# Layer 1's third adaLN projection on VectorE, and its merge with tokens on the partitions

## The chip, the cores and the metric

The kernel runs on one core of a Trainium2 chip. The core has TensorE (PE; its weight loads are shown apart, as PEld), VectorE (DVE), ScalarE (ACT) and GpSimd (POOL). SyncE (SP) issues the DMAs, in order. The metric is the device time of one execution, in microseconds (us). The kernel before takes 1507.12 us, the median of 3 runs (1506.59 to 1509.21).

## The reference

Two layers of a transformer block act on 256 latent tokens and 256 context tokens of width 1024. Each layer is

```
sh1, sc1, g1, sh2, sc2, g2 = split(silu(c) @ w_ada + b_ada, 6)      # adaLN, one row per stream
h = x * (1 + sc1) + sh1
qA, kA, vA, qB, kB, vB, xr, yr, g = split(h @ w_in)
ya = windowed attention(qA, kA, vA);  yb = global attention(qB, kB, vB)
yc = (forward scan + backward scan of a gated recurrence over conv(xr)) * gelu(yr)
ga, gb, gc = split(sigmoid(g), 3)
o = (ga * (ya @ w_br_a) + gb * (yb @ w_br_b) + gc * (yc @ w_br_c)) @ w_out
x = layernorm(ALPHA * x + g1 * o)
x = layernorm(ALPHA * x + g2 * (relu((x * (1 + sc2) + sh2) @ w_ff1) ** 2 @ w_ff2))
```

Layer 1 returns the latent stream alone, so its queries, gates, merge and MLP run on 256 tokens, while layer 0 runs them on 512. All data is fp32.

## The kernel before, in words

**Units.** Each weight is cut into units of up to 1 MB, listed once in `plan_units` in the order of use. A unit is loaded into one of three raw buffers (`emit_dma`), split into a high and a low fp32r part in four pieces (`queue_split`: ScalarE, in the recurrence also VectorE, writes `whi`; VectorE writes `wlo = raw - whi`), and multiplied in three matmuls per 128 rows (high by high, high by low, low by high). `take` hands out a unit; `prefetch` then loads two or three units ahead and queues the split of the next. `tick`, called after every three matmuls, issues one piece at every third call. TensorE waits when a piece that it needs is late.

**Two forms of product.** `cm` keeps a 128x128 block of the weight in TensorE and streams the tokens past it: the result has channels on the partitions, and for layer 1 each matmul streams 256 columns (`LAT`). `unit`, used for `w_out` and `w_ff2`, keeps 128 tokens of the activation in TensorE and streams 512 weight columns: the result has tokens on the partitions. Weights for it are "wide" units of 512 rows by 512 columns.

**adaLN in the background.** A projection of 2048 columns (`ada_queue`) is eight loads of 1 MB into the same three raw buffers. With `dve` set, each load is followed by eight VectorE instructions (the first load by multiplications, line 291, the others by multiply-adds into eight accumulators, line 293), and at the end 16 short matmuls sum over the partitions (`sums`). Without it, TensorE multiplies each load itself in a step of eight recorded matmuls (`mms`). `ada_step`, called at each prefetch, issues the next load once `self.pe`, the kernel's own running estimate of TensorE time at build, has passed `ada_at`, and sets that to `self.pe` plus `ADA_PACE` of the projection's layer (line 326). The adds are issued by `tick` from 3000 ns of that estimate after the load, spread over the rest of the pace; those left over are issued ahead of the next load. `mm` adds 0.42 ns per column to the estimate, so a unit of layer 0's MLP, 48 matmuls of 512 columns, counts 10.3 us. The table `ADA` (line 328) says where a projection is queued: two for layer 1 at the start of layer 0's MLP, and a third (`ga1`, blocks 8 to 11, which give the MLP's scale and gate) on TensorE at layer 1's first gate.

**Layer 1's merge.** While `attention` runs, `pair` fills TensorE's gaps with `filler`: the queries of branch B, then `merge_gates` and `merge_branch` per branch, in the order of `MERGE[1]`. Both use `cm`: 12 gate units of 48 matmuls, four units of 48 for branch c, and eight of 24 for branches a and b, 960 matmuls of 256 columns in all. The gate product goes through a tanh on ScalarE; the branch product is multiplied by it and summed on VectorE, and the sum `m` is split for `wout`. `tail_units` runs the last two `w_out` units and the LayerNorm (`ln_z`), transposes the result (`ln_t`) and makes the MLP's input (`ln_h`).

**Order.** The instructions of an engine stand in one queue, which a scheduler fills at build time; at run time each queue is strictly in order.

Of the kernel before, what the change touches and what calls it, by code (L numbers as in the profile page):

```python
# [9 lines left out]
F32R = mybir.dt.float32r  # L10
AF = mybir.ActivationFunctionType
ALU = mybir.AluOpType
# [3 lines left out]
KD = D // 128  # L16
SEQ = 256
# [9 lines left out]
COL = dict(qA=0, kvA=512, qB=768, kvB=1280, xr=1536, yr=2560, g=3584)  # L27
# [20 lines left out]
class Kern:  # L48
# [95 lines left out]
    def plan_units(self):  # L144
        a, U = self.a, []

        def cols(w, c0, r0=0, k=KD):
            return w[r0:r0 + 128 * k, c0:c0 + 256].rearrange("(k p) c -> p k c", p=128)

        def wide(w, c0, r0):  # L150

            return w[r0:r0 + 512, c0:c0 + 512].rearrange("(k p) c -> p k c", p=128)

        for l in range(DEPTH):
            win = a["w_in"][l]
            order = ("xr0 yr0 xr1 yr1 xr2 yr2 xr3 yr3 kvA qA0 kvB qA1 qB0 qB1",
                     "xr0 xr1 yr0 yr1 kvA xr2 yr2 kvB xr3 yr3 qA0 qA1 qB0 qB1")[l]
            for n in order.split():
                key = (n,) if n[:2] == "kv" else (n[:2], int(n[2]))
                U.append(((l,) + key, cols(win, COL[key[0]] + 256 * sum(key[1:])), KD))  # L160
            for what, br in self.MERGE[l]:
                for n in range(4):
# [12 lines left out]
        self.units = U  # L175
        self.u_dma = self.u_split = 0
        self.u_cur = -1
        self.raw, self.wt = {}, {}
        self.pieces = deque()
# [8 lines left out]
            self.u_dma += 1  # L188

    def is_wide(self, i):  # L190
        return self.units[i][0][1] in ("wo", "f2")

    def shaped(self, t, i):

# [74 lines left out]
    def ada_queue(self, l, blocks, dve):  # L269
# [48 lines left out]
        for k in range(KD):  # L318
            if dve:
                self.ada_q.append((lambda k=k: dma(k),  # L320
                                   [lambda k=k, j=j, s=s: add(k, j, s) for j in range(4) for s in range(2)],
                                   sums if k == KD - 1 else None, self.ADA_PACE[l]))
            else:
                self.ada_q.append((lambda k=k: dma(k), [], lambda k=k: mms(k), 0.0))

    ADA_PACE = (9500, 18000)

    ADA = (('bra0',0,4,1),('bra0',0,8,1),('mlp0',1,0,1),('mlp0',1,4,1),('ga1',1,8,0))

    def ada_start(self, at):  # L330
        for a, l, b, dve in self.ADA:
# [792 lines left out]
    def merge_gates(self, l, br):  # L1124

        cols = BOTH if l == 0 else LAT
        self.tg[br] = []
        for n in range(4):
            w = self.take((l, "g", br, n))
            if br == "c":  # L1130
                if n == 1:
                    while any(step[2] for step in self.bg):
                        self.bg_step()
                    self.y["C"] = []
                    yc = [t for _ in range(KD // 2) for t in self.g2(l, "yc")]
                    for c in range(KD):
                        self.nc.sync.dma_start(out=yc[c][:, cols], in_=self.ycd[c][:, cols])
                elif n > 1:
                    for c in range(4 * n - 8, 4 * n - 4):
                        hi, lo = self.g2(l, "yc_hl", F32R)  # L1140
                        self.split(hi[:, cols], lo[:, cols], yc[c][:, cols], "a")
                        self.y["C"].append((hi, lo))
                    if n == 3:
                        self.flags.add((l, "y", "C"))
            for b, t in enumerate(self.g2(l, "tg")):
                yield from self.cm(w, self.h, cols, b)
                self.act(t[:, cols], self.out, AF.Tanh, scale=0.5)
                self.tg[br].append(t)

    def merge_branch(self, l, br, first, last):  # L1150
        nc = self.nc
        cols = BOTH if l == 0 else LAT
        k = KD if br == "c" else KD // 2
        while (l, "y", br.upper()) not in self.flags:
            yield "need"
        ys = self.y.pop(br.upper())
# [133 lines left out]
    def tail_units(self, l, which, keys, xs):  # L1290


        final = l and which == 2
# [3 lines left out]
            self.hn = [(self.g("h_hi", F32R), self.g("h_lo", F32R)) for _ in range(KD)]  # L1297
        if l:
            ws = []
            for tb, j in ((2, 0), (2, 1), (3, 0), (3, 1)):  # L1300
                if tb == 2:
                    ws.append(self.take(keys[j]))
                self.unit(keys[j], ws[j], xs, (tb,), True)
                if j and not final:
                    self.ln_z(tb)
                elif j:
                    self.output(tb)
# [42 lines left out]
    def wout(self, l):  # L1350
        self.start_residual(l, 1)
        if l == 0:
            self.load_x(l)
        for h in range(2):
            self.unit((l, "wo", 0, h), self.take((l, "wo", 0, h)), self.m_hl(), self.tbs, True)
        self.tail_units(l, 1, [(l, "wo", 1, 0), (l, "wo", 1, 1)], self.m_hl())
        self.m = {}

# [112 lines left out]
    def layer(self, l):  # L1471
        a = self.a
        self.ada_start("layer%d" % l)
        self.layer_consts(l)
        self.ks, self.qs, self.qt, self.vv, self.y, self.m, self.tg, self.qs_at = {}, {}, {}, {}, {}, {}, {}, {}
        self.lru(l)
        if l == 0:
# [122 lines left out]
```

## Time and profile before

| | us |
|---|---|
| median of 3 runs | 1507.12 |
| the profiled execution | 1507.38 |
| its span in the trace | 1505.6 |
| PE busy | 1455.2 |
| DVE busy | 1154.4 |
| ACT busy | 772.2 |
| POOL busy | 292.7 |

The trace covers the span; 1.8 us of the profiled execution's time lie around it. Layer 0's MLP runs from about 575 to 940 us, layer 1's recurrence with its projections from there to about 1109, attention and merge to 1285, `w_out` to 1306, and layer 1's MLP to the end. A busy share counts the time in which an engine had an instruction in work, also where that instruction ran slower than elsewhere.

### The profile page before, as it was taken

Reading aid. Unit: us, or ns where it says so; the run is one execution under the profiler, and the core shown is the slowest. Engines: PE = TensorE matmul, PEld = TensorE weight load, DVE = VectorE, ACT = ScalarE, POOL = GpSimd, SP = SyncE. Lnnn points to the kernel's source line nnn. Section 1 sums busy time; section 2 is a strip of 40 time slices with the busy share of each in tenths; the row PEclk is TensorE's granted clock in tenths of the full one; section 3 lists DMA queues with packets and bytes.
Section 4 is the critical chain, followed back from the end, with each engine's and each line's share of the span. In section 5 each row is a group of like instructions: output and inputs, shape, how many; then the busy total and the mean of one; then the engine's idle time right before and its main releaser. Section 6 shows DMA issues by size and latency. Waiting matters only on the chain.

```text
span 1505.6 us, 22308 instructions
## 1 busy us (share of the span) xinstructions
PE 1455.2 (97%) x8364; PEld 1226.5 (81%) x8364; DVE 1154.4 (77%) x2179; ACT 772.2 (51%) x1594; POOL 292.7 (19%) x298
## 2 busy tenths in 40 slices
PE   7899999999999999899999999999899999899997
PEld 4688988777878879678878887897787899799986
DVE  4699987758688966977657768888989577886666
ACT  2698667565223327313323234587777655655452
POOL 0533422100000002711110301264411003031110
PEclk9999999999999999999999999999999999999999
DMA  9523310105557552444435343342345735755563
GB/s 325 194 85 111 113 57 29 43 29 172 169 190 247 198 198 95 159 160 159 162 112 192 116 168 110 107 143 74 123 144 178 243 109 185 251 169 186 181 193 112
DMA packets 156748, 225.69 MB, mean 150 GB/s; under 512 B 5840, under 2 KB 118992, under 8 KB 151520
## 3 DMA queue, kind: packets, MB, share of 16 engines
q1 hardware_dynamic: 156640, 224.27, 45.2%
q8 instruction: 65, 1.06, 0.3%
q14 instruction: 43, 0.35, 0.1%
HBM read 218.97 MB, written 5.28 MB: 149 GB/s over the span
## 4 chain that ended last, share of the span: by engine, by line
PE 80%; DVE 12%; ACT 4%; issue 2%; DMA 1%; POOL 0%; SPq 0%; DVEq 0%; ACTq 0%
PE ps_cm L92 42%; PE ps_tm L92 26%; DVE wlo L128 3%; PE ps_s L92 2%; PE ps_pv L92 2%; PE ps_pT L99 2%; PE ps_ada L92 2%; PE ps_gate L92 2%; DVE ada_acc L293 1%; DVE xc L647 1%; DMA raw_ada<-in_w_ada_dram 1%; PE ps_qT L99 1%; ACT L103 1%; DVE lru_q L718 1%; DVE lru_i L708 0%
## 5 line engine op out<-in xcount | busy, mean ns | idle before, releaser
L120 ACT CAST whi<-raw 128x512 fp32r<-128x512 f32 x521 | 300.1, 622 | 374.0 <-PE ps_tm L92 195.3
L128 DVE TENSOR_TENSOR wlo<-raw,whi 128x512 fp32r<-128x512 f32 x560 | 407.0, 753 | 103.2 <-ACT whi L120 98.0
L92 PE MATMUL ps_cm<-h_hi,wlo 128*128 128x256 f32 (+1 forms) x1216 | 406.9, 337 | 7.0 <-DVE wlo L128 6.9
L92 PE MATMUL ps_cm<-h_hi,whi 128*128 128x256 f32 (+1 forms) x1216 | 408.5, 340 | 3.0 <-ACT whi L120 2.0
L92 PE MATMUL ps_cm<-h_lo,whi 128*128 128x256 f32 (+1 forms) x1216 | 406.1, 336 | 0.2 <-POOL h_lo L1249 0.2
L92 PEld LDWEIGHTS ps_cm<-h_hi,whi 128*128 128x128 f32 x1216 | 230.4, 191 | 39.9 <-ACT whi L120 7.1
L92 PEld LDWEIGHTS ps_cm<-h_hi,wlo 128*128 128x128 f32 x1216 | 231.9, 191 | 34.3 <-DVE wlo L128 9.2
L92 PEld LDWEIGHTS ps_cm<-h_lo,whi 128*128 128x128 f32 x1216 | 232.0, 191 | 24.1 <-POOL h_lo L1249 0.7
L293 DVE SCALAR_TENSOR_TENSOR ada_acc<-raw_ada,silu,ada_acc 128x512 f32<-128x512 f32 x224 | 168.7, 799 | 49.6 <-DMA raw_ada<-in_w_ada_dram 49.4
L92 PE MATMUL ps_tm<-wlo,f_hi 128*128 128x512 f32 x384 | 150.2, 392 | 2.1 <-DVE wlo L128 2.1
L92 PE MATMUL ps_tm<-whi,f_hi 128*128 128x512 f32 x384 | 149.7, 390 | 0.0
L92 PE MATMUL ps_tm<-whi,f_lo 128*128 128x512 f32 x384 | 149.3, 389 | 0.0
L1188 POOL TENSOR_TENSOR x<-x,res 128x512 f32<-128x512 f32 x36 | 51.9, 1445 | 306.8 <-DVE res L1187 306.8
L92 PE MATMUL ps_tm<-wlo,h_hi 128*128 128x256 f32 x320 | 92.0, 287 | 6.1 <-DVE wlo L128 6.0
L92 PE MATMUL ps_tm<-whi,h_hi 128*128 128x256 f32 x320 | 92.9, 290 | 1.2 <-ACT lru_r L103 0.6
L92 PE MATMUL ps_tm<-whi,h_lo 128*128 128x256 f32 x320 | 91.4, 286 | 0.0
L92 PEld LDWEIGHTS ps_tm<-wlo,f_hi 128*128 128x128 f32 x384 | 72.1, 188 | 19.6 <-DVE wlo L128 5.2
L92 PEld LDWEIGHTS ps_tm<-whi,f_hi 128*128 128x128 f32 x384 | 72.1, 188 | 15.7 <-ACT whi L120 0.8
L103 ACT ACTIVATE p<-ps_s,mx 128x512 f32<-128x512 f32 (+1 forms) x96 | 58.5, 618 | 51.2 <-DVE mx L1001 29.9
L92 PEld LDWEIGHTS ps_tm<-whi,f_lo 128*128 128x128 f32 x384 | 72.1, 188 | 14.8
L685 POOL TENSOR_TENSOR lru_i<-lru_i,xc 128x512 f32<-128x512 f32 x32 | 52.8, 1680 | 89.3 <-ACT lru_i L103 89.3
L92 PEld LDWEIGHTS ps_tm<-wlo,h_hi 128*128 128x128 f32 x320 | 62.0, 194 | 7.7 <-DVE wlo L128 7.3
(173 smaller groups left out, 2449.5 us busy)
## 6 DMA issues: line engine op xcount, KB each, us to landing
raw<-in_w_ff_dram SPq DMA_DIRECT2D x64, 1024.0 KB, 5.5
raw<-in_w_in_dram SPq DMA_DIRECT2D x50, 1024.0 KB, 5.1
raw_ada<-in_w_ada_dram SPq DMA_DIRECT2D x40, 1024.0 KB, 5.0
w_ada<-in_w_ada_dram SPq DMA_DIRECT2D x32, 256.0 KB, 5.6
raw<-in_w_br_c_dram SPq DMA_DIRECT2D x8, 1024.0 KB, 5.7
raw<-in_w_out_dram SPq DMA_DIRECT2D x8, 1024.0 KB, 5.0
gw_raw<-in_v_gate_dram SPq DMA_DIRECT2D x16, 256.0 KB, 5.3
raw<-in_w_br_a_dram SPq DMA_DIRECT2D x8, 512.0 KB, 3.5
```

What stands on the lines that cost most here:

```text
L92: self.nc.tensor.matmul(out, lhsT, rhs, start=start, stop=stop, **kw)
L99: self.nc.tensor.transpose(out, in_, self.ident if n == 128 else self.ident[0:n, 0:n])
L103: ins = self.nc.scalar.activation(out, in_, func, **kw).ins
L120: self.nc.scalar.copy(out, in_)
L128: return self.nc.vector.tensor_tensor(lo, src, hi.bitcast(F32), op=ALU.subtract)
L293: self.nc.vector.scalar_tensor_tensor(acc, w, c, acc, op0=ALU.mult, op1=ALU.add)
L647: nc.vector.scalar_tensor_tensor(o, r3[:, :, lo_ + d:lo_ + d + n], w(j), o, op0=ALU.mult, op1=ALU.add)
L685: nc.gpsimd.tensor_tensor(ig, ig, self.xc[k[0]][0], op=ALU.mult)
L718: nc.vector.tensor_tensor_scan(h[:, cs][:, ::-1], r[:, cs][:, ::-1], ig[:, cs][:, ::-1], init, op0=ALU.mult, op1=ALU.add)
L1188: (nc.vector if last else nc.gpsimd).tensor_tensor(x, x, t, op=ALU.add)
```

## The change

The third projection of layer 1 is queued behind the other two at the start of layer 0's MLP, on VectorE, and the pace of layer 1's projections is 12000 ns in place of 18000. Layer 1's gate and branch weights become wide units: `tw` keeps 128 tokens in TensorE and streams 512 weight columns (480 matmuls in place of 960), so gates, branch products and their sum have tokens on the partitions. `merge_t` transposes the sum once, 16 blocks of 128x128 on TensorE into PSUM, half of it in the middle of the last branch unit and half in the middle of the first `w_out` unit, and splits it from there. In layer 1's last `w_out` units the order over token blocks and units changes.

```diff
@@ plan_units, is_wide
+                if l:
+                    for n in range(2):
+                        for h in range(2 if what == "g" or br == "c" else 1):
...
+                            U.append(((l, what, br, n, h), src, KD))
+                    continue
-        return self.units[i][0][1] in ("wo", "f2")
+        l, what = self.units[i][0][:2]
+        return what in ("wo", "f2") or l and what in ("g", "br")
@@ adaLN
-    ADA_PACE = (9500, 18000)
+    ADA_PACE = (9500, 12000)
-    ADA = (('bra0',0,4,1),('bra0',0,8,1),('mlp0',1,0,1),('mlp0',1,4,1),('ga1',1,8,0))
+    ADA = (('bra0',0,4,1),('bra0',0,8,1),('mlp0',1,0,1),('mlp0',1,4,1),('mlp0',1,8,1))
@@ merge_gates
+            if l:
+                if n % 2 == 0:
+                    po = {}
+                for tb in (2, 3):
+                    yield from self.tw(w, self.h, tb, n % 2, 2, po)
+                    if n % 2:
+                        t = self.g("tg")
+                        self.act(t, po.pop(tb), AF.Tanh, scale=0.5)
+                        self.tg[br].append(t)
+                continue
+    def tw(self, w, xs, tb, h, n_h, po):
+        whi, wlo = w
+        if h == 0:
+            po[tb] = self.ps("ps_tw")
+        o, ts = po[tb], slice(128 * tb, 128 * tb + 128)
+        for i in range(4):
+            xhi, xlo = xs[4 * h + i]
+            self.mm(o, xhi[:, ts], whi[:, i, :], h == 0 and i == 0, False)
+            self.mm(o, xhi[:, ts], wlo[:, i, :], False, False)
+            self.mm(o, xlo[:, ts], whi[:, i, :], False, h == n_h - 1 and i == 3)
+            self.tick()
+            yield
+    def merge_tokens(self, l, br, first, last):
...
+                for tb in (2, 3):
+                    yield from self.tw(w, ys, tb, h, n_h, po)
+                    if last and n and tb == 2:
+                        self.merge_t(0)
...
+                    nc.vector.scalar_tensor_tensor(t, t, 1.0, po.pop(tb), op0=ALU.add, op1=ALU.mult)
...
+                        nc.vector.tensor_tensor(self.m[i], self.m[i], t, op=ALU.add)
+    def merge_t(self, n):
+        for j in range(2):
+            p = self.ps("ps_m")
...
+                    self.tp(p[:, 256 * b + 128 * tb:256 * b + 128 * tb + 128], self.m[2 * n + tb][:, c:c + 128])
+            hi, lo = self.g("m_hl", F32R), self.g("m_hl", F32R)
+            self.split(hi, lo, p)
...
@@ tail_units, wout
-            for tb, j in ((2, 0), (2, 1), (3, 0), (3, 1)):
+            for tb, j in ((2, 0), (2, 1), (3, 0), (3, 1)) if final else ((2, 0), (3, 0), (2, 1), (3, 1)):
+            if l and h == 0:
+                self.unit((l, "wo", 0, h), w, self.mt, (2,), True)
+                self.merge_t(1)
...
+                self.unit((l, "wo", 0, h), w, self.m_hl(), (3,), True)
```

How the queues change is shown at three places. On SP, from the LayerNorm's stores (`xd`) at the start of layer 1 on: `raw` is a weight unit, `raw_ada` a load of a projection, `gw_raw` a gate weight of the recurrence, `ycd` its result. Before:

```order
L1270 DMA xd<-x 128x512 x4
L186 DMA raw<-in_w_in_dram 128x8x256
L628 DMA gw_raw<-in_v_gate_dram 128x512 x2
L186 DMA raw<-in_w_in_dram 128x8x256 x2
L628 DMA gw_raw<-in_v_gate_dram 128x512 x2
L186 DMA raw<-in_w_in_dram 128x8x256 x2
L731 DMA ycd<-lru_q 128x256 x2
```

And now:

```order
L1344 DMA xd<-x 128x512 x4
L287 DMA raw_ada<-in_w_ada_dram 128x2048
L196 DMA raw<-in_w_in_dram 128x8x256
L639 DMA gw_raw<-in_v_gate_dram 128x512 x2
L196 DMA raw<-in_w_in_dram 128x8x256
L287 DMA raw_ada<-in_w_ada_dram 128x2048
L639 DMA gw_raw<-in_v_gate_dram 128x512 x2
L196 DMA raw<-in_w_in_dram 128x8x256 x2
L287 DMA raw_ada<-in_w_ada_dram 128x2048
L196 DMA raw<-in_w_in_dram 128x8x256
L742 DMA ycd<-lru_q 128x256 x2
```

The third projection's loads stand in layer 1's recurrence: one of the eight stands ahead of this piece, three are in it, four follow.

On DVE, around the second batch of the recurrence in layer 1: `xc` is the convolution, `lru_q` and `lru_i` the recurrence's terms, `wlo` and `whi` weight pieces. Before:

```order
L122 CAST whi<-raw 128x512 x2
L128 TENSOR_TENSOR xc_lo<-xc,xc_hi 128x512
L128 TENSOR_TENSOR wlo<-raw,whi 128x512 x3
L700 SCALAR_TENSOR_TENSOR lru_q<-lru_q,lru_th 128x512 x4
L128 TENSOR_TENSOR wlo<-raw,whi 128x512
L885 TENSOR_REDUCE ss<-sq 128x2 x2
L122 CAST whi<-raw 128x512 x2
L708 TENSOR_TENSOR lru_i<-lru_i,lru_q 128x512 x4
```

And now:

```order
L304 SCALAR_TENSOR_TENSOR ada_acc<-raw_ada,silu,ada_acc 128x512
L128 TENSOR_TENSOR wlo<-raw,whi 128x512
L304 SCALAR_TENSOR_TENSOR ada_acc<-raw_ada,silu,ada_acc 128x512 x4
L711 SCALAR_TENSOR_TENSOR lru_q<-lru_q,lru_th 128x512 x2
L304 SCALAR_TENSOR_TENSOR ada_acc<-raw_ada,silu,ada_acc 128x512 x2
L711 SCALAR_TENSOR_TENSOR lru_q<-lru_q,lru_th 128x512 x2
L304 SCALAR_TENSOR_TENSOR ada_acc<-raw_ada,silu,ada_acc 128x512
L896 TENSOR_REDUCE ss<-sq 128x2 x2
L122 CAST whi<-raw 128x512
L719 TENSOR_TENSOR lru_i<-lru_i,lru_q 128x512 x4
```

Eight adds stand among the batch's own instructions. Of the 64 instructions of the third projection, 15 stand on DVE ahead of the first whole convolutions of layer 1, 9 between those and the end of the first batch, and 40 from there to the first scores.

On PE, at the end of the merge: `ps_cm` and `ps_tw` are products of the merge, `ps_m` the transposes, `ps_tm` the first `w_out` unit. Before:

```order
L92 MATMUL ps_cm<-y_hl,whi 128x256 x2
L92 MATMUL ps_cm<-y_hl,wlo 128x256
L92 MATMUL ps_tm<-whi,m_hl 128x512
L92 MATMUL ps_tm<-wlo,m_hl 128x512
```

And now:

```order
L92 MATMUL ps_tw<-whi,y_hl 128x512
L99 MATMUL ps_m<-ident,tg 128x128 x8
L92 MATMUL ps_tw<-whi,y_hl 128x512
L92 MATMUL ps_tw<-wlo,y_hl 128x512
...
L92 MATMUL ps_tm<-whi,m_hl 128x512
L99 MATMUL ps_m<-ident,tg 128x128 x8
L92 MATMUL ps_tm<-whi,m_hl 128x512
```

Two groups of eight transposes were added, twelve matmuls of 512 columns apart from the products that read them or lead to them.

## Rows read from the trace of the kernel before

**Rows 1.** The page's part 1: busy time, share of the span, instructions.

```profile
PE 1455.2 (97%) x8364; PEld 1226.5 (81%) x8364; DVE 1154.4 (77%) x2179; ACT 772.2 (51%) x1594; POOL 292.7 (19%) x298
```

**Rows 2.** Busy time by stretch; the first line names the columns.

```profile
core 0: us, PE busy (x) PEld busy (x) DVE busy (x) ACT busy (x) POOL busy (x), PEclk, DMA share, GB/s
933.00:1109.00 176.00, 161.96 (x1080) 145.11 (x1079) 152.91 (x266) 125.09 (x236) 73.47 (x76) 0.98 0.34 113
940.00:970.00 30.00, 27.73 (x224) 25.92 (x216) 22.75 (x54) 15.26 (x35) 8.90 (x9) 1.00 0.33 113
970.00:1006.00 36.00, 35.90 (x246) 33.40 (x247) 32.32 (x55) 31.98 (x58) 13.78 (x9) 1.00 0.41 136
1006.00:1109.00 103.00, 91.33 (x578) 81.01 (x577) 92.21 (x153) 71.20 (x132) 46.38 (x53) 0.97 0.34 109
1109.00:1160.00 51.00, 48.81 (x351) 39.77 (x350) 48.20 (x125) 44.17 (x101) 4.94 (x9) 0.97 0.52 171
1160.00:1285.00 125.00, 125.00 (x1010) 113.92 (x1009) 86.23 (x190) 71.61 (x163) 15.31 (x11) 1.00 0.56 183
640.00:920.00 280.00, 279.52 (x1238) 228.69 (x1239) 192.88 (x311) 79.19 (x144) 34.55 (x24) 1.00 0.46 152
```

**Rows 3.** DVE's waits, 933 to 1109: us in total, times, longest us.

```profile
DVE lru_q L700 <- ACT lru_q L694: 5.0, 4, 3.0
DVE whi L122 <- PE ps_tm L92: 4.9, 3, 3.1
DVE h_lo L1249 <- ACT h_hi L1247: 3.6, 4, 1.4
```

**Rows 4.** SP's queue in order of time: start us, us, instruction.

```profile
875.52 0.34 SPq L276 DMA_DIRECT2D raw_ada<-in_w_ada_dram  x1
...
897.35 0.34 SPq L276 DMA_DIRECT2D raw_ada<-in_w_ada_dram  x1
...
1101.59 0.33 SPq L276 DMA_DIRECT2D raw_ada<-in_w_ada_dram  x1
```

**Rows 5.** Instructions by form: busy us, mean ns, idle before and its releaser.

```profile
L293 DVE SCALAR_TENSOR_TENSOR ada_acc<-raw_ada,silu,ada_acc 128x512 f32<-128x512 f32 x224 | 168.7, 799 | 49.6 <-DMA raw_ada<-in_w_ada_dram 49.4
...
L291 DVE TENSOR_SCALAR ada_acc<-raw_ada,silu 128x512 f32<-128x512 f32 x32 | 15.5, 516 | 0.0
```

**Rows 6.** DVE in order of time, start of layer 0's MLP: start us, us.

```profile
585.01 0.88 DVE L291 TENSOR_SCALAR ada_acc<-raw_ada,silu 128x512 f32<-128x512 f32 x2
...
629.32 3.47 DVE L293 SCALAR_TENSOR_TENSOR ada_acc<-raw_ada,silu,ada_acc 128x512 f32<-128x512 f32 x2
...
634.31 2.73 DVE L293 SCALAR_TENSOR_TENSOR ada_acc<-raw_ada,silu,ada_acc 128x512 f32<-128x512 f32 x4
```

**Rows 7.** The chain of waits, 900 to 1345: start us, us, what.

```profile
1171.97 1.00 PE ps_ada L92 x8
...
1258.84 25.75 PE ps_cm L92 x213
1284.59 16.36 PE ps_tm L92 x72
```

**Rows 8.** PE in order of time, three places: start us, us; idle before.

```profile
938.60 1.92 PE L92 MATMUL ps_ada<-ada_acc,pick 128*32 128x512 f32 x16
...
1306.22 1.03 PE L99 MATMUL ps_z<-ident,x 128*128 128x128 f32 x8
1311.11 1.47 PE L99 MATMUL ps_z<-ident,x 128*128 128x128 f32 x8 [3.86 <-DVE x L1226]
```

**Rows 9.** DVE in order of time at the end of `w_out`.

```profile
1306.43 1.29 DVE L128 TENSOR_TENSOR wlo<-raw,whi 128x512 fp32r<-128x512 f32 x2
1307.63 0.68 DVE L1187 TENSOR_TENSOR res<-ps_tm,gate 128x512 f32<-128x512 f32 x1
...
1310.65 1.38 DVE L1226 TENSOR_SCALAR x<-x,mv,rstd 128x256 f32<-128x256 f32 x4
```

**Rows 10.** POOL in order of time, start of layer 0's MLP: start us, us.

```profile
605.70 26.54 POOL L1268 TENSOR_TENSOR x<-x,ln_row 128x512 f32<-128x512 f32 x16 [13.97 <-DMA ln_row<-in_ln_g_dram]
```

**Rows 11.** PE's waits, 570 to 670: us in total, times, longest us.

```profile
PE ps_cm L92 <- DVE wlo L128: 2.2, 1, 2.2
PE ps_tm L92 <- DVE wlo L128: 2.1, 4, 1.4
```

More of the change, by code (lines that the diff above doesn't have):

```diff
@@ L161, in plan_units @@
             for what, br in self.MERGE[l]:
+                if l:
+                    for n in range(2):
+                        for h in range(2 if what == "g" or br == "c" else 1):
+                            if what == "g":
+                                src = wide(win, COL["g"] + 1024 * "abc".index(br) + 512 * n, 512 * h)
+                            else:
+                                src = wide(a["w_br_" + br][l], 512 * n, 512 * h)
+                            U.append(((l, what, br, n, h), src, KD))
+                    continue
                 for n in range(4):
@@ L1128, in merge_gates @@
         for n in range(4):
-            w = self.take((l, "g", br, n))
+            w = self.take((l, "g", br, n) if l == 0 else (l, "g", br, n // 2, n % 2))
             if br == "c":
@@ L1148, in merge_gates @@
                 self.tg[br].append(t)
+    def tw(self, w, xs, tb, h, n_h, po):
[11 more added lines that the diff above has]
+    def merge_tokens(self, l, br, first, last):
+        nc = self.nc
+        ys = self.y.pop(br.upper())
+        n_h = len(ys) // 4
+        for n in range(2):
+            po = {}
+            for h in range(n_h):
+                w = self.take((l, "br", br, n, h))
+                for tb in (2, 3):
+                    yield from self.tw(w, ys, tb, h, n_h, po)
+                    if last and n and tb == 2:
+                        self.merge_t(0)
+                    if h < n_h - 1:
+                        continue
+                    i = 2 * n + tb - 2
+                    t = self.tg[br][i]
+                    nc.vector.scalar_tensor_tensor(t, t, 1.0, po.pop(tb), op0=ALU.add, op1=ALU.mult)
+                    if first:
+                        self.m[i] = t
+                    else:
+                        nc.vector.tensor_tensor(self.m[i], self.m[i], t, op=ALU.add)
+    def merge_t(self, n):
+        for j in range(2):
+            p = self.ps("ps_m")
+            for b in range(2):
+                for tb in range(2):
+                    c = 128 * (2 * j + b)
+                    self.tp(p[:, 256 * b + 128 * tb:256 * b + 128 * tb + 128], self.m[2 * n + tb][:, c:c + 128])
+            hi, lo = self.g("m_hl", F32R), self.g("m_hl", F32R)
+            self.split(hi, lo, p)
+            self.mt += [(Lat(hi, 0), Lat(lo, 0)), (Lat(hi, SEQ), Lat(lo, SEQ))]
     def merge_branch(self, l, br, first, last):
@@ L1155, in merge_branch @@
             yield "need"
+        if l:
+            yield from self.merge_tokens(l, br, first, last)
+            return
         ys = self.y.pop(br.upper())
@@ L1354, in wout @@
         for h in range(2):
-            self.unit((l, "wo", 0, h), self.take((l, "wo", 0, h)), self.m_hl(), self.tbs, True)
+            w = self.take((l, "wo", 0, h))
+            if l and h == 0:
+                self.unit((l, "wo", 0, h), w, self.mt, (2,), True)
+                self.merge_t(1)
+                self.m = dict(enumerate(self.mt))
+                self.mt = []
+                self.unit((l, "wo", 0, h), w, self.m_hl(), (3,), True)
+            else:
+                self.unit((l, "wo", 0, h), w, self.m_hl(), self.tbs, True)
         self.tail_units(l, 1, [(l, "wo", 1, 0), (l, "wo", 1, 1)], self.m_hl())
@@ L1474, in layer @@
         self.layer_consts(l)
+        self.mt = []
         self.ks, self.qs, self.qt, self.vv, self.y, self.m, self.tg, self.qs_at = {}, {}, {}, {}, {}, {}, {}, {}
```

## The prediction

> **What bounds the kernel now.** Part 1 of the page comes first: TensorE is busy for 97% of the span [rows 1]. That is an average, so the table of stretches is read next [rows 2], and there three stages differ. In layer 0's MLP (640 to 920) TensorE is busy for 279.5 of 280 us and VectorE for 192.9: TensorE binds, and VectorE has 87 us free. In layer 1's recurrence (933 to 1109) VectorE is busy for 152.9 of 176 us, while GpSimd works for 73.5. What is left of VectorE there, 23.1 us, comes in short waits for ScalarE and TensorE, the longest 3.1 us [rows 3]. VectorE binds this stage. From 1160 to 1285, attention and merge, TensorE is busy for 125 of 125 us and VectorE for 86.2: TensorE binds again. So a TensorE instruction saved in the merge is worth its time, and a VectorE instruction costs nothing in the MLP but nearly its time in the recurrence.
>
> **The third projection: where it lands.** The words of the change put it into layer 0's MLP. The code issues one load per prefetch at most, once the estimate has passed the pace. A unit counts 10.3 us, so a pace of 18 us and one of 12 us both mean every second unit. The trace shows that: loads at 875.52 and 897.35 are 21.8 us apart, and the one at 897.35 is the last of the sixteen of the first two projections, at the MLP's end [rows 4]. The MLP has no room for eight more. The order agrees: the new loads stand between the first weights of layer 1 and its first gate unit, and all 64 VectorE instructions stand in the recurrence, 15, 9 and 40 in the three stretches 940 to 970, 970 to 1006 and 1006 to 1109 [rows 2]. In the kernel before, nothing of a projection ran there: after 897.35 the next load is at 1101.59 [rows 4].
>
> **What they cost.** The 224 multiply-adds take 168.7 us, 0.753 each, and the 32 multiplications 15.5, 0.484 each [rows 5]. For 56 and 8 that is 42.2 + 3.9 = 46.1 us, the value I take, since it mixes quiet GpSimd and busy GpSimd as the recurrence does. With GpSimd quiet four adds take 2.73 us, 0.68 each, and two multiplications 0.88 [rows 6]: 38.2 + 3.5 = 41.7, the low end. For the high end, the adds of a load can stand waiting for it, with everything behind them in the queue: 49.6 us over 28 loads [rows 5], 1.8 each, for eight loads 14.2, in all 60.3.
>
> Some of it falls into VectorE's idle time. The three stretches leave 7.3, 3.7 and 10.8 us [rows 2], 21.8 in all, if every gap had an add ready. The order puts 15 instructions around the waits for `h_hi` and eight around the wait for `lru_q`, which are the gaps in rows 3, but others stand where there is none. I take 14 us hidden (7.3 of the first stretch, the 3 to 4 us at `lru_q`, 3 of the rest). The recurrence grows by 46.1 - 14 = 32 us, between 41.7 - 21.8 = 20 and 60. It can't be made up: behind each add stand weight pieces and convolutions, which TensorE needs within the next unit, so the delay passes to TensorE, and TensorE has no reserve in the merge behind.
>
> **What TensorE gets back.** The projection on TensorE was eight steps of 1.00 us [rows 7]; the sums that take their place are 16 matmuls in 1.92 us [rows 8]: 6.1 us less. The 960 merge matmuls of 256 columns come every 25.75/213 = 0.1209 us, 116.1 us in all; 480 of 512 columns come every 16.36/72 = 0.2272 us [rows 7], 109.1 us. That is 7.0 us less, or 7.7 at the 279.52/1238 = 0.2258 us of the MLP [rows 2]. The gain is in the fixed part of each matmul, as the columns streamed are the same.
>
> Of the Trainium skill's TensorE: Matmul & The Clock Gate, the section Back-to-back issue gap gives an isolated gap of N/2.4 + 2.5 ns. By that the two forms would take 104.8 and 103.6 us, an estimate from that page, and the merge would gain 1.2 us in place of 7.0. The same section names about 131 ns per matmul of 512 columns for a sustained stream, which the trace contradicts with 227 ns. The rows decide.
>
> The 16 transposes cost 1.03/8 = 0.129 us each [rows 8], 2.1 us. Their operands and splits are covered: between the first eight and the first `w_out` matmul stand 12 matmuls, 2.7 us at 0.2272, and the same again around the second eight, against a cast, a subtraction and the merge's own two VectorE steps. If the cover fails, TensorE waits 1 to 2 us once. ScalarE's and VectorE's evacuations become half as many and twice as wide, in a stage where neither binds: nothing.
>
> **The rest.** The new order of the last `w_out` units starts the first token block's normalisation 5.4 us later but moves two weight pieces out of the way that delayed the second block (1306.43 to 1307.63) [rows 9]. TensorE's wait of 3.86 us [rows 8] ends about where it does now: 0, between -1 and +2. The shorter pace moves the second load of layer 0's MLP one unit forward, ahead of the weights of the fourth `w_ff1` unit on SP, and its eight adds into the stretch where GpSimd works on `x` [rows 10] and TensorE already waits 4.3 us for weight pieces [rows 11]. I take 0, between -4 (that wait goes) and +6 (eight adds at 0.75 more). In the rest of that MLP the earlier adds cost nothing, covered by the 87 us. The prefetch stays at two units instead of three through the recurrence; SP's queue then holds a weight behind each load. That is inside the high end above.
>
> **Sum,** on the profiled execution's own 1507.38 us (span 1505.6; the median of the runs is 0.26 lower): + 32 - 6.1 - 7.0 + 2.1 = +21.0, so 1528.
>
> **Rivals.**
> (a) The adds cost far more. While GpSimd works, two adds take 3.47 us, 1.74 each, in place of 0.68 [rows 6, 10]. GpSimd is busy for 73.5 of the 176 us, 42%: then an add costs 0.58 x 0.68 + 0.42 x 1.74 = 1.13 us, the 64 together 66.5, the stage grows by 52.5, and the time is 1549. The Trainium skill's GPSIMD Engine Reference (Specifications) says that GpSimd shares its SBUF interfaces with VectorE and contends with VectorE instructions that have two SBUF inputs; the adds have two, and the trace agrees. Against it: GpSimd's own 76 instructions in that stage stay as many, so most of the waiting that they cause is in VectorE's 152.9 us already.
> (b) The adds displace only what can wait. A third of VectorE's work in the recurrence (scans, their products) isn't needed before branch c of the merge, and could slide past 1109, where VectorE is idle for 2.8 + 38.8 us [rows 2] and TensorE runs on. The change is faster if the recurrence grows by less than 11.0 us, the sum of TensorE's terms. With the low price (20) and 13 us slid, it grows by 7, and the time is 1503. For it: the gaps [rows 3] are waits, not work. Against it: the queue is in order, and pieces of weights stand behind the adds.
> (c) Nothing to tell: growth and gain cancel within 3 us, 1507.
> That the third projection runs in layer 0's MLP at all is ruled out by the order.
>
> **How the numbers follow.** Forecast 0.62, (a) 0.20, (b) 0.13, (c) 0.05. The forecast's own ends are 1507.4 + 20 - 11.7 - 4 = 1512 and 1507.4 + 60 - 11 = 1556; with (a) inside and (c) at its lower edge I give 1506 to 1553, which leaves out (b) and the forecast's top, together just under 0.2. A difference of 0.2%, 3 us, is about what a measurement of this kernel can tell from none. Slower: forecast and (a), less a little for their low edges, 0.81. Faster: (b), 0.13. Within: (c) and the edges, 0.06.
>
> **What would show it.** Right: `raw_ada` loads on SP between layer 1's first weights and its first gate; 64 more VectorE instructions and VectorE over 90% busy in the recurrence, that stage some 30 us longer, TensorE waiting there for `wlo`; 480 matmuls `ps_tw` about 0.227 us apart, the merge 10 to 12 us shorter, no `ps_ada` steps in it. Wrong: a recurrence less than 11 us longer, with adds in gaps or scans after the first scores (b); adds of over 1 us each (a); TensorE waiting for `ps_m` at the first `w_out` unit, or for PSUM banks in the merge, since two are now held across two units; a different clock: TensorE's granted clock is 0.97 to 0.98 of 2.4 GHz in the recurrence and just after [rows 2], and longer waits could lower it.

## The result and the profile after

The changed kernel takes 1527.9 us, the median of 4 runs (1526.86 to 1529.71), against 1506.86 for the kernel before: a ratio of 1.0138, 95% interval 1.012 to 1.0155. It is slower by 21.0 us; 1528 was forecast. The profiled execution took 1528.46 us, its span 1526.5. That the total came out within a microsecond is luck: two terms missed by 4 and 3 us in opposite directions, as the stages show.

Part 1 of the page after, which answers to [rows 1]:

```profile
PE 1455.6 (95%) x7852; PEld 1208.2 (79%) x7852; DVE 1200.5 (79%) x2219; ACT 770.1 (50%) x1578; POOL 303.4 (20%) x298
```

TensorE has 512 instructions fewer and is not busy for less time; VectorE is busy for 46 us more. That says nothing yet of where the 21 us are. For that the span is cut at instructions that both kernels have: the first transposes of layer 0's first and last LayerNorm, the first query transpose of layer 1's attention, and the first `w_out` matmul. From TensorE's timeline of the kernel before (start us, us, instruction):

```profile
562.09 1.03 PE L99 MATMUL ps_z<-ident,x 128*128 128x128 f32 x8
...
925.45 1.03 PE L99 MATMUL ps_z<-ident,x 128*128 128x128 f32 x8
...
1097.07 0.72 PE L99 MATMUL ps_qT<-ident,qstk 128*128 128x128 f32 x4
...
1284.43 0.40 PE L92 MATMUL ps_tm<-whi,m_hl 128*128 128x512 f32 x1
```

And of the changed kernel, with the last LayerNorm's transposes as well ([rows 8] has those of before, at 1311.11):

```profile
561.53 1.03 PE L99 MATMUL ps_z<-ident,x 128*128 128x128 f32 x8
...
927.32 1.03 PE L99 MATMUL ps_z<-ident,x 128*128 128x128 f32 x8
...
1126.62 0.61 PE L99 MATMUL ps_qT<-ident,qstk 128*128 128x128 f32 x4
...
1304.88 0.39 PE L92 MATMUL ps_tm<-whi,m_hl 128*128 128x512 f32 x1
...
1330.41 1.60 PE L99 MATMUL ps_z<-ident,x 128*128 128x128 f32 x8 [2.71 <-DVE x L1300]
1332.38 1.97 PE L99 MATMUL ps_z<-ident,x 128*128 128x128 f32 x8 [0.37 <-DVE x L1300]
```

| stage | before | after | change | forecast |
|---|---|---|---|---|
| layer 0's MLP | 363.36 | 365.79 | +2.4 | 0 |
| layer 1's recurrence | 171.62 | 199.30 | +27.7 | +32 |
| attention and merge | 187.36 | 178.26 | -9.1 | -6.1 - 7.0 + 1.0 = -12.1 |
| `w_out` to the last transposes | 26.68 | 27.50 | +0.8 | +1.0 |
| the rest | | | -0.9 | 0 |
| span | 1505.6 | 1526.5 | +20.9 | +21 |

The recurrence first. Busy time by stretch (the columns as in [rows 2]), the kernel before, recurrence and then attention with the merge:

```profile
925.45:1097.07 171.62, 157.87 (x1030) 140.07 (x1029) 145.91 (x249) 121.55 (x229) 72.79 (x73) 0.98 0.31 103
1097.07:1284.43 187.36, 184.88 (x1444) 164.29 (x1444) 144.70 (x339) 122.58 (x277) 22.95 (x23) 0.99 0.55 179
```

The changed kernel, the same two, and then the busy time of the projections' instructions alone (their only engine here is VectorE) in the recurrence and behind it:

```profile
927.32:1126.62 199.30, 167.08 (x1040) 149.11 (x1039) 189.69 (x311) 122.73 (x230) 79.60 (x73) 0.93 0.39 129
1126.62:1304.88 178.26, 173.86 (x915) 132.75 (x915) 144.14 (x322) 119.03 (x261) 22.29 (x23) 1.00 0.44 148
```

```profile
927.30:1126.60 199.30, 46.84 (x61) 0.93 0.39 129
1126.60:1300.00 173.40, 2.21 (x3) 1.00 0.44 149
```

VectorE goes from 145.91 of 171.62 us to 189.69 of 199.30, from 85% to 95%. Of the 64 instructions 61 lie in the stage, 46.84 us. VectorE's idle time shrinks from 25.7 to 9.6 us, so 16.1 us are hidden. VectorE's busy time grows by 43.8 us, and 43.8 - 16.1 = 27.7, the growth. The 3.1 us between 46.84 and 43.8 are not work that moved away: the stage's other VectorE instructions are 250 (249 before), and in a full queue an instruction's record begins before the last one's ends, as in the rows below (1116.07 for 0.74 us, the next at 1116.73). GpSimd has the same 73 instructions. Seen from TensorE the 27.7 us are 18.5 us more of idle time (13.75 to 32.22) and 9.2 us more of busy time.

How the adds reach TensorE is seen at the end of the stage. VectorE's timeline of the changed kernel:

```profile
1116.07 0.74 DVE L304 SCALAR_TENSOR_TENSOR ada_acc<-raw_ada,silu,ada_acc 128x512 f32<-128x512 f32 x1
1116.73 0.41 DVE L737 TENSOR_TENSOR lru_q<-lru_q,yr 128x256 f32<-128x256 f32 x1
1117.07 3.39 DVE L304 SCALAR_TENSOR_TENSOR ada_acc<-raw_ada,silu,ada_acc 128x512 f32<-128x512 f32 x5
1120.38 0.68 DVE L128 TENSOR_TENSOR wlo<-raw,whi 128x512 fp32r<-128x512 f32 x1
```

Six adds stand ahead of a weight piece. TensorE's timeline at the same place, with the wait in brackets:

```profile
1121.11 0.58 PE L92 MATMUL ps_tm<-wlo,h_hi 128*128 128x256 f32 x1 [6.52 <-DVE wlo L128]
1121.49 0.42 PE L92 MATMUL ps_tm<-whi,h_lo 128*128 128x256 f32 x1
1121.71 0.41 PE L92 MATMUL ps_tm<-whi,h_hi 128*128 128x256 f32 x1
...
1127.30 0.29 PE L92 MATMUL ps_tm<-whi,h_lo 128*128 128x256 f32 x1
1127.42 0.28 PE L92 MATMUL ps_tm<-whi,h_hi 128*128 128x256 f32 x1
```

TensorE waits 6.52 us for that piece. Behind the wait its matmuls of 256 columns come 0.22 us apart, and from 1127 on 0.12. The granted clock (the number behind the five busy times) says why:

```profile
1114.50:1121.00 6.50, 0.10 (x1) 0.00 (x0) 6.50 (x12) 0.00 (x0) 0.45 (x1) 0.91 0.50 155
1121.00:1127.00 6.00, 5.89 (x30) 5.89 (x30) 5.71 (x13) 3.70 (x8) 1.62 (x2) 0.53 0.55 177
1127.00:1133.00 6.00, 4.95 (x40) 4.58 (x38) 5.42 (x13) 2.46 (x3) 2.15 (x3) 1.00 0.56 185
```

It fell while TensorE stood idle (busy for 0.10 of 6.50 us). For 6 us it is then 0.53 of 2.4 GHz, near the lower level of 1.2, and after that the full one again. TensorE's waits in the whole stage, 927 to 1127 (us in total, times, longest us):

```profile
PE ps_tm L92 <- DVE wlo L128: 10.9, 5, 6.5
PE ps_cm L92 <- DVE wlo L128: 8.8, 4, 3.5
PE ps_tm L92 <- ACT whi L120: 3.8, 2, 3.4
```

And in the kernel before, 925 to 1097:

```profile
PE ps_tm L92 <- DVE wlo L128: 6.0, 5, 2.8
PE ps_cm L92 <- DVE wlo L128: 1.6, 1, 1.6
```

The waits for `wlo` are 19.7 us, where the kernel before had 7.6 in its stage.

### The profile page after: what moved, and what is told of

Read it like the earlier page. It is cut to its first block, busy times and chain, and to the rows that moved or that the text cites. A ratio compares the mean times of both kernels' runs of the same rounds, so it can differ in the third digit from the quotient of the medians.

```text
span 1526.5 us, 21281 instructions
## 1 busy us (share of the span) xinstructions
PE 1455.6 (95%) x7852; PEld 1208.2 (79%) x7852; DVE 1200.5 (79%) x2219; ACT 770.1 (50%) x1578; POOL 303.4 (20%) x298
## 4 chain that ended last, share of the span: by engine, by line
PE 77%; DVE 14%; ACT 3%; issue 3%; DMA 1%; POOL 1%; SPq 0%; DVEq 0%; ACTq 0%; POOLq 0%
PE ps_cm L92 35%; PE ps_tm L92 25%; PE ps_tw L92 6%; DVE wlo L128 4%; PE ps_pv L92 2%; PE ps_s L92 2%; PE ps_pT L99 2%; DVE ada_acc L304 2%; PE ps_ada L92 2%; PE ps_gate L92 1%; DVE xc L658 1%; DVE lru_q L729 1%; DMA raw<-in_w_ff_dram 1%; ACT L103 1%; ACT p L103 1%
## 5 line engine op out<-in xcount | busy, mean ns | idle before, releaser
L128 DVE TENSOR_TENSOR wlo<-raw,whi 128x512 fp32r<-128x512 f32 x560 | 412.2, 763 | 94.6 <-ACT whi L120 92.8
L92 PE MATMUL ps_cm<-h_hi,wlo 128*128 128x512 f32 (+1 forms) x1024 | 353.8, 349 | 15.9 <-DVE wlo L128 15.9
L92 PE MATMUL ps_cm<-h_hi,whi 128*128 128x512 f32 (+1 forms) x1024 | 354.8, 351 | 5.4 <-ACT whi L120 2.0
L92 PE MATMUL ps_cm<-h_lo,whi 128*128 128x512 f32 (+1 forms) x1024 | 353.1, 347 | 0.8 <-DVE h_lo L1323 0.7
L304 DVE SCALAR_TENSOR_TENSOR ada_acc<-raw_ada,silu,ada_acc 128x512 f32<-128x512 f32 x280 | 213.1, 804 | 65.3 <-DMA raw_ada<-in_w_ada_dram 65.3
L92 PEld LDWEIGHTS ps_cm<-h_hi,wlo 128*128 128x128 f32 x1024 | 196.2, 193 | 43.2 <-DVE wlo L128 18.6
L92 PEld LDWEIGHTS ps_cm<-h_hi,whi 128*128 128x128 f32 x1024 | 196.1, 193 | 33.5 <-ACT whi L120 3.8
L92 PEld LDWEIGHTS ps_cm<-h_lo,whi 128*128 128x128 f32 x1024 | 197.2, 193 | 24.0 <-DVE h_lo L1323 1.1
L1262 POOL TENSOR_TENSOR x<-x,res 128x512 f32<-128x512 f32 x36 | 56.8, 1585 | 299.3 <-DVE res L1261 299.3
L92 PEld LDWEIGHTS ps_tm<-whi,h_hi 128*128 128x128 f32 x320 | 63.9, 200 | 6.1 <-ACT whi L120 4.2
```

The costliest lines, as they stand in the source:

```text
L92: self.nc.tensor.matmul(out, lhsT, rhs, start=start, stop=stop, **kw)
L128: return self.nc.vector.tensor_tensor(lo, src, hi.bitcast(F32), op=ALU.subtract)
L304: self.nc.vector.scalar_tensor_tensor(acc, w, c, acc, op0=ALU.mult, op1=ALU.add)
L1262: (nc.vector if last else nc.gpsimd).tensor_tensor(x, x, t, op=ALU.add)
```

## The experiments

All are ratios to the kernel before, run on the same chip as the version, with 95% intervals. They were run in three sets on three chips (first the two parts alone, the adds cut and the pace of 10000; then the adds doubled, the even spread and the groups of six; then the rest), so ratios compare better across sets than times. What is said of stages comes from one trace of each version.

**The merge alone.**

```diff
-    ADA_PACE = (9500, 12000)
+    ADA_PACE = (9500, 18000)
-    ADA = (..., ('mlp0',1,4,1),('mlp0',1,8,1))
+    ADA = (..., ('mlp0',1,4,1),('ga1',1,8,0))
```

> The changed kernel with the projections' table and pace of the kernel before: the third projection is multiplied by TensorE at layer 1's first gate again; the wide merge units, the transposes and the new order of the last w_out units stay. Theory (the terms of the prediction): 1506.9 - 7.0 + 2.1 = 1502 us, between 1500 and 1504. Rival (the matmuls of 512 columns save hardly anything beside attention, or a wait for the transposes takes it): 1506 to 1509. The profile of layer 1's recurrence should be that of the kernel before.

Measured: 1505.73 us against 1508.1, ratio 0.9982 (0.9973 to 0.9992). A gain of 2.7 us (0.0018 of 1508), 1.2 to 4.1, where 4.9 was forecast. The time misses the theory's 1500 to 1504 and lies just under the rival's 1506, so the rival, hardly any gain, is only just out. The recurrence is that of before (172.4 us). Attention and merge take 184.4 in place of 187.4 us, forecast 6.0 less.

**The projection alone.**

```diff
-    ADA_PACE = (9500, 18000)
+    ADA_PACE = (9500, 12000)
-    ADA = (..., ('mlp0',1,4,1),('ga1',1,8,0))
+    ADA = (..., ('mlp0',1,4,1),('mlp0',1,8,1))
```

(in the kernel before)

> The kernel before with the new table and pace alone: the third projection on VectorE, the merge as it was. Theory (VectorE binds the recurrence): 1506.9 + 32 - 6.1 = 1533 us, between 1528 and 1537. Rival (the merge's wide units are what costs, by their waits for weight pieces): under 1515.

Measured: 1529.57 against 1508.1, ratio 1.0138 (1.0125 to 1.0152): 20.8 us slower, the same as the whole change; the two intervals are too wide to show the merge's 2.7 us between them. Its recurrence takes 197.8 us, 26.2 more; attention and merge give back 3.7. So the loss is the projection's, and the rival falls: the old merge does not avoid it. The time grows by some 5 us less than the 26 expected: the recurrence grows by 26 in place of 32, while attention and merge give back 2.4 us less than the 6.1.

**The adds cut to eight columns.**

```diff
+                n = 8 if l and blocks[0] == 8 else 512
-                self.nc.vector.scalar_tensor_tensor(acc, w, c, acc, op0=ALU.mult, op1=ALU.add)
+                self.nc.vector.scalar_tensor_tensor(acc[:, 0:n], w[:, 0:n], c, acc[:, 0:n], op0=ALU.mult, op1=ALU.add)
```

> The changed kernel with the 56 multiply-adds of the third projection cut to 8 columns each in place of 512, so most of that projection is left out; its loads, their places in SP's queue, the two-unit prefetch, the eight multiplications and the sums stay. Theory (VectorE's time is the cost): most of the growth goes, 1500 to 1505 us. Rival (the loads ahead of weights and the shorter prefetch delay the pieces): over 1518 us, nearly the changed kernel's 1527.9.

Measured: 1506.8 against 1508.1, ratio 0.9992 (0.9983 to 1.0001), so the adds' width is worth 1.0138 - 0.9992, 22 us. Loads and the shorter prefetch stayed, and their rival is out. It is 2 us over the expected range, and a row shows what was left. The instructions by form (busy us, mean ns):

```profile
L305 DVE SCALAR_TENSOR_TENSOR ada_acc<-raw_ada,silu,ada_acc 128x8 f32<-128x8 f32 x56 | 15.9, 344 | 1.8 <-DMA raw_ada<-in_w_ada_dram 1.8
```

The 56 narrow adds still take 15.9 us; the projection keeps 20 of its 49 us of VectorE, and the recurrence is 4.6 us longer than in the kernel before.

**The adds doubled.**

```diff
+                for _ in range(2 if l and blocks[0] == 8 else 1):
-                self.nc.vector.scalar_tensor_tensor(acc, w, c, acc, op0=ALU.mult, op1=ALU.add)
+                    self.nc.vector.scalar_tensor_tensor(acc, w, c, acc, op0=ALU.mult, op1=ALU.add)
```

> The changed kernel with each of the 56 multiply-adds of the third projection issued twice (its sums are then wrong). Theory (VectorE is full in the recurrence, 190 of 199 us, so that 56 more of 0.767 us = 43 us find at most its last 9.6 us of idle time): 1528 + 34 to 43 = 1562 to 1571 us. Rival (adds go on finding gaps as those of the change did, 16 of 44 us): 1528 + 27 = 1555 us or less.

Measured: 1563.26 against 1507.52, ratio 1.0368 (1.0354 to 1.0382): 0.0230 above the changed kernel's ratio, 35 us. The rival's 27 is out, and the value lies in the theory's range, near its lower end. The recurrence and its projection instructions:

```profile
927.19:1149.58 222.39, 176.06 (x1043) 155.38 (x1042) 215.72 (x351) 119.93 (x223) 84.72 (x73) 0.88 0.34 113
```

```profile
927.19:1149.58 222.39, 86.67 (x104) 0.88 0.34 113
1149.58:1300.00 150.42, 11.61 (x16) 0.95 0.41 135
```

VectorE is busy for 97%. The reason differs in part from the one expected: the second 56 adds took 98.28 - 49.05 = 49.2 us, not 43, and 16 instructions fell behind the stage, where attention and merge became 11 us longer. So 35 of 49 us were paid, against 28 of 49 for the first ones. Part of the 35 may be TensorE at its lower clock: granted were 0.88 in the recurrence and 0.95 in the 150 us behind it, where the changed kernel has 0.93 and 1.00.

**All 24 loads in layer 0's MLP, one per unit.**

```diff
-    ADA_PACE = (9500, 12000)
+    ADA_PACE = (9500, 10000)
```

> The changed kernel with a pace of 10000 ns for layer 1's projections, under the 10.3 us that a unit counts: one load per unit, so that all 24 loads and their adds lie in layer 0's MLP. Theory (VectorE's 87 free us of that stage cover the 46): the recurrence is that of the kernel before, and 1506.9 - 6.1 - 7.0 + 2.1 = 1496 us, up to 1500. Rival (in the stretch with a load at every unit VectorE is busy for about 97%, weight pieces come late, and the MLP of layer 0 grows by 10 us or more): 1506 us or more.

Measured: 1519.37 against 1508.1, ratio 1.0069 (1.0055 to 1.0083). The recurrence is that of before again (172.0 us), but the MLP takes 386.9 us, 23.5 more: the rival is right. TensorE's waits there, 570 to 960:

```profile
PE ps_ada L92 <- DVE ada_acc L304: 7.9, 2, 4.3
PE ps_tm L92 <- DVE wlo L128: 6.3, 4, 3.9
```

Adds that are left over are issued ahead of the next load, and at a projection's end its sums follow at once: 7.9 us of TensorE waiting for adds. The kernel before waits 4.3 us in its MLP. With a wait of 0.5 us for `h_lo` these are 10.4 us more, less than half of the 23.5. Most of the rest are the sums themselves; over the MLP, TensorE's busy time in `ps_ada` and, in brackets, its matmuls:

```profile
563.21:950.13 386.92, 11.67 (x48) 0.98 0.49 160
```

The kernel before has 16 of these matmuls in its MLP, 1.92 us. The 9.8 us more come from their number and from their pace: behind its wait a matmul of the sums took 1.06 us in place of 0.62, and the granted clock of the stage is 0.98 (1.00 before). Some 3 us stay open.

**The 24 loads spread evenly.** Three loads in four units, the next due 13000 ns after the last was due; the second version also has the adds 600 ns apart.

```diff
-    ADA_PACE = (9500, 12000)
+    ADA_PACE = (9500, 13000)
-            self.ada_at, self.ada_next, self.ada_gap = self.pe + pace, self.pe + 3000, (pace - 3000) / 8
+            at = self.ada_at + pace if pace > 10000 and self.ada_at + 2 * pace > self.pe else self.pe + pace
+            self.ada_at, self.ada_next, self.ada_gap = at, self.pe + 3000, (pace - 3000) / 8
```

In the second version the last term is `600.0 if pace > 10000 else (pace - 3000) / 8`.

> The changed kernel with the 24 loads spread evenly over layer 0's MLP: a pace of 13000 ns counted from the time at which the last load was due, not from when it was issued, which gives three loads in four units. Theory (VectorE's free time of that stage covers the adds when they are spread, and the sums no longer wait for adds issued just ahead of them): the recurrence as in the kernel before, 1508 - 6.1 - 2.7 (the merge alone as measured) = 1499 us, between 1496 and 1503. Rival (any denser loading holds back weights for want of raw buffers, and the MLP grows by half of what the pace of 10000 cost, 12 us): 1508 to 1512.

> As the even spread of 24 loads over layer 0's MLP, with the adds of a load issued 600 ns apart in place of 1250, so that all eight are issued before the next load also where that comes one unit later. Theory (leftover adds ahead of a load delay it and what follows): 2 to 5 us under the same spread with adds 1250 ns apart. Rival (adds close together delay the weight pieces): 2 us or more above it.

Measured: 1505.13 against 1507.52, 0.9983 (0.9974 to 0.9992), and 1503.79, 0.9976 (0.9966 to 0.9985). Both miss their ranges: the first lies 2 us above the theory and 3 below its rival, and the two versions can't be told apart. The MLP is 371.0 and 371.1 us, 7.7 longer than before. In the second version attention and merge get 7.2 us shorter than with the merge alone, by the steps that leave TensorE. What the projection gives there it takes here (in the first version 3.5 us of TensorE's idle time, and 48 matmuls of sums in place of 16, 3.9 us): spread this way it costs nothing and earns nothing that can be told.

**The shorter pace alone.** The merge alone, with the pace of 12000 for the two projections in the MLP.

```diff
-    ADA = (..., ('mlp0',1,4,1),('mlp0',1,8,1))
+    ADA = (..., ('mlp0',1,4,1),('ga1',1,8,0))
```

> The merge change alone, with the pace of 12000 ns for the two projections that stay in layer 0's MLP. Theory (the prediction's term for the shorter pace, 0 between -4 and +6; the MLP of layer 0 was 2.4 us longer in the changed kernel's trace): 1505 to 1508 us, with the MLP of layer 0 between 363 and 366 us. Rival (those 2.4 us belong to the third projection's loads, not to the pace): 363.4 us for that MLP, and the time of the merge change alone.

Measured: 1507.57 against 1507.66, 0.9999 (0.999 to 1.0007), in the theory's range; the MLP is 364.55 us, 1.2 above the merge alone. By the ratios this version is 2.6 us slower than the merge alone, and the two intervals only just overlap. Five traces have the pace of 12000 (363.5 for the projection alone, 364.2 with the adds doubled, 364.6 here, 365.8 in the changed kernel, 366.2 with the adds cut), five that of 18000 (363.0 to 363.4). So the pace costs the MLP 1.7 us on the mean, 0.1 to 3.3 between single traces. Where it does is shown by 626 to 642, in the kernel before and in the changed one:

```profile
626.00:642.00 16.00, 12.31 (x48) 8.64 (x49) 15.96 (x21) 4.41 (x8) 6.24 (x4) 1.00 0.37 111
626.00:642.00 16.00, 11.32 (x36) 8.59 (x37) 15.97 (x16) 1.54 (x3) 10.38 (x7) 0.79 0.27 77
```

VectorE is full in both. In the changed kernel TensorE is idle for 1 us more there, its granted clock is 0.79 in place of 1.00, and it gets 36 matmuls done in place of 48.

**The merge in groups of six.** The merge alone, where `tw` hands over to attention after six matmuls.

```diff
             self.tick()
-            yield
+            if i % 2:
+                yield
```

> The merge change alone (third projection on TensorE as before), with the merge's matmuls handed to the attention in groups of six in place of three. Theory (the first wide matmul behind a group of short ones takes 0.31 to 0.34 us to the next in place of 0.23, and half of the groups go): some 30 changes fewer at 0.1 us, 3 us less, 1503 us against 1505.7 for groups of three. Rival (attention's own steps come later, and TensorE waits for them): 1506 us or more.

Measured: 1501.98 against 1507.52, 0.9965 (0.9951 to 0.9979), 2.6 us under the 0.9982 of groups of three, though the two intervals overlap a little; 1503 was expected, from 1505.7. From the first query to the first `w_out` matmul it takes 181.4 us (184.4). The cause is only in part the one expected. What a change of group costs shows in the merge alone:

```profile
1163.07 0.60 PE L99 MATMUL ps_pT<-ident,p 128*128 128x128 f32 x4
1163.43 0.48 PE L92 MATMUL ps_tw<-whi,h_hi 128*128 128x512 f32 x1
1163.74 0.40 PE L92 MATMUL ps_tw<-wlo,h_hi 128*128 128x512 f32 x1
1163.97 0.40 PE L92 MATMUL ps_tw<-whi,h_lo 128*128 128x512 f32 x1
```

The first wide matmul behind four transposes takes 0.31 us to the next, the second 0.23. But the changes of this kind fell only from 54 to 44, not by 30, which is 1 us. TensorE's waits of the stage fell by 1.2 us more (1.8 for `wlo` and 1.1 for `pT` went, 1.8 for `qstk` came). The remaining microsecond is the clock's, which the edit doesn't touch. The first 2 us of the stage, with groups of three and of six:

```profile
1097.61:1099.61 2.00, 2.00 (x11) 2.00 (x11) 1.71 (x4) 1.17 (x2) 1.20 (x2) 0.51 0.55 130
1096.58:1098.58 2.00, 2.00 (x20) 2.00 (x18) 2.00 (x6) 1.33 (x3) 0.00 (x0) 1.00 0.00 0
```

With groups of three TensorE still ran at the lower level there (0.51), behind the end of the recurrence. So the groups themselves earned about 2 us of the 3 in these traces.

**Groups of twelve, the old order of the tail, and both changes together.** Groups of twelve have `if i == 3` in that line. The old tail takes the condition out again, in groups of six:

```diff
-            for tb, j in ((2, 0), (2, 1), (3, 0), (3, 1)) if final else ((2, 0), (3, 0), (2, 1), (3, 1)):
+            for tb, j in ((2, 0), (2, 1), (3, 0), (3, 1)):
```

The last has groups of six and the even spread with adds 600 ns apart.

> The merge change alone with groups of twelve matmuls. Theory (fewer changes between long and short matmuls, and the gain goes on): 1499 to 1501 us. Rival (attention's steps come too late, its own chain through ScalarE and VectorE becomes the bound): 1504 us or more.

> The merge change alone in groups of six, with the last w_out units in the order of the kernel before. Theory (the prediction's term for the order of the tail, 0 between -1 and +2): 1501 to 1504 us, no difference that can be told from 1502. Rival (the new order is what earns the merge change its gain): 1505 us or more.

> Both changes in the best form found: 24 loads spread over layer 0's MLP with adds 600 ns apart, and the merge in groups of six. Theory (the gains are in different stages and add): 1507.5 - 3.7 (the spread with the merge) - 3.8 (groups of six) = 1500 us, 1498 to 1502. Rival (groups of six only save waits that the spread version doesn't have): 1503 us or more.

Measured against 1507.66: twelve 1502.82, 0.9965 (0.9952 to 0.9977), no further gain, between theory and rival; the old tail 1500.79, 0.9961 (0.9948 to 0.9973), as expected no difference (from `w_out` to the last transposes 27.55 us, 27.50 with the new order); both together 1501.18, 0.9957 (0.9943 to 0.997), in the expected range. These four versions with larger groups lie within each other's intervals. They beat the kernel before by 5 to 6.5 us and the changed one by 25 to 27, and groups of six with the projection left on TensorE are the smallest edit that does.

## Why the prediction was right

**Where it lands.** As forecast. SP's queue has the first load of the third projection at the MLP's end and the other seven in the recurrence; the first two and the last:

```profile
908.71 0.35 SPq L287 DMA_DIRECT2D raw_ada<-in_w_ada_dram  x1
...
953.26 0.33 SPq L287 DMA_DIRECT2D raw_ada<-in_w_ada_dram  x1
...
1103.34 0.34 SPq L287 DMA_DIRECT2D raw_ada<-in_w_ada_dram  x1
```

**What the adds cost.** The mechanism was right: VectorE bound the stage, and the delay reached TensorE through weight pieces. Cutting the adds took the loss away, doubling them brought 35 us more. The size was 4 us too high, half of it each way: the instructions raised VectorE's busy time in the stage by 43.8 us (46.1 forecast), and 16.1 us were hidden (14 forecast). The 64 took 49.05 us by their records, but three of them, 2.2 us, fell behind the stage, and the records of the others overlap with their neighbours'. **Rival (b)** is out: it needed a growth under 11 us, and it was 27.7; three adds were all that slid, and none of the stage's other work did.

**Rival (a)** is out: an add of the changed kernel's recurrence took 0.77 us (46.84/61, with the multiplications), not 1.13. Single ones were slowed beside GpSimd (1.78 us at 995.46, while a GpSimd subtraction ran from 995.07 for 1.62); the mean hardly was. The Trainium skill's GPSIMD Engine Reference (Specifications) holds for those, but gave no size.

**What TensorE gets back** was 3 us too high, 9.1 in place of 12.1. In the stage's two rows TensorE's busy time falls by 11.0 us, and its idle time grows by 1.9 (2.48 to 4.40). The busy time falls by 7.6 us for `ps_ada` (9.56 to 1.92; 6.1 forecast) and by 4.5 for the products (131.26 us for 960, 126.78 for 480; 7.0 forecast), and the eight transposes in the stage add 1.0. About 1.8 us of it is the clock, 0.99 in the stage before and 1.00 in the changed kernel, and no term of the sum. The rows of the projection alone and the merge alone:

```profile
1124.22:1307.85 183.63, 177.29 (x1387) 160.64 (x1387) 146.43 (x341) 121.26 (x276) 21.54 (x23) 1.00 0.43 139
1097.61:1282.02 184.41, 181.08 (x972) 135.62 (x972) 142.36 (x320) 119.56 (x262) 23.14 (x23) 0.99 0.55 186
```

By themselves they gave 3.7 and 3.0 us, where 6.1 and 6.0 were forecast, and together 9.1: the two gains are not independent. With the projection alone TensorE is busy for 7.6 us less, but its idle time grows by 3.9 us (2.48 to 6.34), in waits for ScalarE's `p` and VectorE's `qstk` among others; with the wide merge in place the same steps give 6.1 (184.41 to 178.26, 1.0 of it the clock). So one step that fell short is "a TensorE instruction saved in the merge is worth its time": beside attention part of it comes back as waits. Why more of it does without the wide merge is open. The other is the products, 4.5 us of 7.0.

The rate that the sum used for the merge, 0.2272 us from 72 in a row [rows 7], nearly held. The chain of waits of the changed kernel, late in its merge:

```profile
1284.36 1.88 PE ps_pv L92 x16
1286.23 15.19 PE ps_tw L92 x66
```

That is 0.230 each for a row of 66, its first one, behind attention's products, included; at 0.230 480 take 110.5 us and save 5.6, not 7.0. The median from start to start, within rows, is 0.227 us, and 0.120 for 256 columns in the kernel before. Behind a group of attention's the next start comes 0.08 to 0.11 us later than within a row in both kernels (0.20 to 0.22 and 0.31 to 0.34 us), so that doesn't tell the two forms apart. The rate thus explains 0.8 to 1.4 of the 2.5 us; the rest was not separated. Of the Trainium skill's TensorE: Matmul & The Clock Gate (Back-to-back issue gap) both figures stay off: 1.2 us of gain, estimated from its isolated gap, against 4.0 for the merge alone in that stage (3.0 and the 1.03 us of the eight transposes in it; some 0.8 of it is the clock), and its 131 ns against 0.227 us.

**The transposes** cost about what was forecast (0.87 us for eight on the chain, 1.03 forecast), and their cover held: TensorE goes from the products to the transposes and on to `w_out` without a wait. **The tail** came out as forecast: waits of 2.71 and 0.37 us in place of 3.86, and no difference when the old order was put back. **The pace** was taken at 0 and cost 1.7 us on the mean of the traces, inside the -4 to +6 given.

## What to carry to other kernels

Work "for a background engine" costs nothing only in the stage where that engine has time, so look where the queue really puts it: here the pace rounded to whole units and pushed the adds of eight loads into the one stage in which VectorE was already 85% busy. Of the work added to the binding engine 56 and 71% was paid here, since its idle time is gaps that such work fills only in part. And matmuls saved beside a second stream are worth less than their own time: some of it comes back as waits between the two, so two such gains have to be measured together, not added. Look at the granted clock of a stage before a difference of 1 or 2 us is put down to the edit.

## What was not expected of the hardware

A wait of TensorE cost more than its length: behind the 6.52 us the granted clock was 0.53 for 6 us, and 256 columns took 0.21 to 0.22 us in place of 0.12. Over the recurrence the granted clock was 0.93 (0.98 before), and TensorE was busy for 9.2 us more with ten instructions more. The clock explains that: 0.07 of 199.3 us against 0.02 of 171.6 is some 10 us of TensorE's time lost. How much of it reached the end was not separated; it can't be more than the 9.6 us in which VectorE was idle, as VectorE was busy for the other 189.7 us of the stage.

A VectorE multiply-add of 8 columns took 15.9/56 = 0.28 us on the mean, but that mixes two cases. From the kernel with the adds cut to eight columns, VectorE and GpSimd where they work side by side, and then VectorE with GpSimd idle:

```profile
988.12 6.04 DVE L305 SCALAR_TENSOR_TENSOR ada_acc<-raw_ada,silu,ada_acc 128x8 f32<-128x8 f32 x8
986.97 6.15 POOL L697 TENSOR_TENSOR lru_i<-lru_i,xc 128x512 f32<-128x512 f32 x4 [3.93 <-ACT lru_i L103]
1078.59 1.17 DVE L305 SCALAR_TENSOR_TENSOR ada_acc<-raw_ada,silu,ada_acc 128x8 f32<-128x8 f32 x8
```

With GpSimd idle eight take 1.17 us, 0.15 each. Beside GpSimd four of the eight took 1.25 to 1.34 us each, and GpSimd's last three instructions there 1.30 each, in turn with them. So the narrow adds cost that much for their company and not for their width: the 512 columns of the one at 995.46 in the changed kernel took 1.78.
